# Conditioning rows of a two-block network: sums on VectorE alone, and the second layer's rows made in block 2's first feed-forward phase

## The chip, the cores and the metric

The kernel runs on one core of one Trainium2 chip. The metric is the device time of one execution in microseconds; three executions of the kernel before took 3672.66, 3673.09 and 3675.40 us, so 3673.09 in the median.

## What is computed (the reference)

A network of two blocks on 512 tokens of width 1024. Block 1 has two layers; each is a mixer (attention over dilated windows, a convolution and a pooling branch, gated and summed), a cross-attention over 256 memory tokens, and a feed-forward part with a causal convolution. Block 2 has two layers as well, on the same 512 tokens and on 256 context tokens. It is conditioned: from a vector c for the tokens and one c_ctx for the context come, per layer, six rows of 1024 each that shift, scale and gate the block's norms:

```python
for l in range(DEPTH):
    mx = (silu(c) @ ada_w[l] + ada_b[l]).reshape(bsz, 6, 1, d)
    mc = (silu(c_ctx) @ ada_w[l] + ada_b[l]).reshape(6, d)
    hx = modulate(rmsnorm_2(x, norm_g[l, 0]), mx[:, 0], mx[:, 1])
    ...                                      # mixer: yx, yc
    x = x + mx[:, 2] * rmsnorm_2(yx, norm_g[l, 1])
    hx = modulate(rmsnorm_2(x, norm_g[l, 2]), mx[:, 3], mx[:, 4])
    x = x + mx[:, 5] * rmsnorm_2(swiglu(hx, ffn_w13[l], ffn_w2[l]), norm_g[l, 3])
    ...                                      # the same for the context, with mc
```

The rows depend on c, c_ctx and the weights `ada_w` (2 x 1024 x 6144) alone, so they can be made at any time before block 2's layer uses them. All products are in float32, by splitting each operand into a high and a low part in TensorE's float32r format and adding three products.

## The kernel before

**Phases.** `run` (L1487) goes through block 1's phases `mix1`, `mem1`, `ffn1` twice, then block 2: `mix_ab`, `ffn2(0)`, `mix_mla`, `ffn2(1)`. In the feed-forward phases PSUM is four tiles of two banks (`open_ring`, L99). Every weight unit, 128 x 1024, comes through `wload` (L122): a DMA on SP's queue into one of three `raw` tiles, a copy to the high part on ScalarE (`whi`, L109), a subtraction for the low part on VectorE (`wlo`, L112), in one of five pairs of tiles. `mm3` (L133) is the three matmuls of a product. The compiler lays each engine's instructions in an order of its own, by the program's order and by what it holds to be ready; steps without a dependence on each other may be exchanged.

**A feed-forward phase** (`ffn1`, L826; `ffn2`, L1275) has 22 hidden chunks of 128, handled in parts of three to six chunks. For each chunk, two weight units are multiplied with the feature-major input (`projT`), the two results are combined (block 1: convolution at L530 and L533, Silu at L863, product at L865; block 2: Silu at L1314 and L1317, products at L1315 and L1318), and the result is split into `act` or `a` (L109 on ScalarE, L112 on VectorE). At the end of a part, `out_part` (L252) multiplies the part's chunks, for each token tile, with the rows of the down matrix, and VectorE adds the result to the running sums (L262). This is a part boundary: the first tile's last matmuls need the last chunk's `act`. `up_lead` (L815) makes the first two chunks' products while the input's tiles still come. With the last part come the norm and the residual's update (`postnorm`, L190), and the next phase's input.

**The conditioning rows** are made in `ffn1` by `ada_rows` (L908), in layer l of block 1 for layer l of block 2. One part is one of the six rows, for c and c_ctx at once. Per part, eight weight tiles `adaw` of 128 x 1024 come over SP's queue into two buffers, and two accumulators `acc0` (c) and `acc1` (c_ctx) take the tile times a number per partition:

```python
if kc == 0:
    nc.vector.tensor_scalar(acc[0], w, c[0], 1.0, op0=ALU.mult, op1=ALU.mult)           # L919
    nc.gpsimd.tensor_scalar(acc[1], w, c[1], 1.0, op0=ALU.mult, op1=ALU.mult)           # L920
else:
    nc.vector.scalar_tensor_tensor(acc[0], w, c[0], acc[0], op0=ALU.mult, op1=ALU.add)  # L922
    p = pool.tile([P, D], F32, name="adap")
    nc.gpsimd.tensor_scalar(p, w, c[1], 1.0, op0=ALU.mult, op1=ALU.mult)                # L924
    nc.gpsimd.tensor_tensor(acc[1], acc[1], p, op=ALU.add)                              # L925
```

Then TensorE sums over the partitions with four matmuls against ones (L938; 96 instructions in the profile over all parts), VectorE adds the bias (L939) and, for scales and gates, takes in the norm's gain (L941), and four small DMAs store the row in DRAM (L944). `mod_row` and `mod_col` (L947, L952) read it back where a phase needs it.

**What paces them.** `Fill` (L40) holds the generator. Each `yield 1` is one step and costs 1; after each chunk from the third on, `fill.run(3)` (L876) emits steps until what they cost is paid. A part is nine steps, a phase has 20 x 3 to pay with and 54 steps; what is left is drained before the last part's `out_part` (L879).

**The residual** `x` (four tiles of 128 x 1024) and, in block 2, `xc` (two tiles) lie on the right side of SBUF. `spill_x` (L285) stores them in DRAM and frees the room where a mixer needs it, `open_x` (L278) takes it again and loads them. In the feed-forward phases they stay in SBUF, though they are only read and written at the phase's two ends: `postnorm` adds to them as the last part's sums come.

Of the kernel before, what the change touches and what calls it, by code (L numbers as in the profile page):

```python
# [11 lines left out]
F32 = mybir.dt.float32  # L12
# [5 lines left out]
ALU = mybir.AluOpType  # L18
# [21 lines left out]
class Fill:  # L40
    """Work for TensorE, by key, that is laid between the steps of something with longer waits."""
# [37 lines left out]
class Net:  # L79
# [14 lines left out]
    def psum_pools(self, ctx, **bufs):  # L94
        """PSUM tiles under names of their own: of two banks for ps and S, of one for others."""
        pool = self.pool(ctx, "psum", space=PSUM)
        self.banks = {tag: (pool, n) for tag, n in bufs.items()}

    def open_ring(self):  # L99
        """All of PSUM as four tiles of two banks, from the end of one mixer to the next one."""  # L100
        self.ringctx = ExitStack()
        self.psum_pools(self.ringctx, ps=4)
# [19 lines left out]
    def wload(self, src, pool=None):  # L122
        """A weight unit as its two float32r parts."""
# [9 lines left out]
    def mm3(self, ps, l, r, first, last):  # L133
        """ps += l.T @ r, of operands that are given as (hi, lo)."""
# [10 lines left out]
    def rstd(self, src, n=D, junk=None):  # L145
        """1 / sqrt(mean of squares + eps) along the free axis."""
# [11 lines left out]
    def at(self, hT, t):  # L158
        """Columns of token tile t of (hi, lo), or of (hi, lo, hi, lo) with the context's tiles 4 and 5 apart."""
# [5 lines left out]
    def to_T(self, src, hT, t, shift=None, whole=False):  # L165
        """[128 tokens, 1024] -> columns t of the feature-major (hi, lo); shift [128, 8] is added by feature."""
# [23 lines left out]
    def postnorm(self, x, y, g, psum=False, last=False):  # L190
        """x += rmsnorm(y) * g"""
# [16 lines left out]
    def lead1(self, name, l):  # L208
        """The normalised and feature-major input of a phase, and what makes token tile t of it."""
# [5 lines left out]
    def lead2(self, l, i, hT, gp=None):  # L215
        """The same for block 2; hT may be what the phase before still reads other tiles of."""
# [11 lines left out]
    def ending(self, post, pre, lag=1):  # L228
        """What takes a phase's sums by token tile: the next phase's tiles begin as the residual's come,
        the last ones between that phase's first products."""  # L230
# [9 lines left out]
    def ready(self, t):  # L240
        """Token tile t of the phase's input, and those before it."""
# [3 lines left out]
    def projT(self, ps, unit, hT, kcs, col=0, n=S, w=P, off=0, first=True, last=True):  # L245
        """Feature-major product: ps[w, n] of a weight unit's columns and hT."""
# [5 lines left out]
    def out_part(self, acts, wsrc, tiles, yps, first, last, epi):  # L252
        """Token-major product of some feature chunks with the rows [128, 1024] of a matrix that belong
        to them; parts add up in yps, and epi(t, y) takes a tile's whole sum."""
# [30 lines left out]
    def spill_x(self, write=True):  # L285
        """Frees the tiles; returns where the residual comes back from."""
# [7 lines left out]
    def open_xc(self):  # L294
# [3 lines left out]
        for t in range(2):  # L298
            self.nc.sync.dma_start(self.xc[t], self.I["ctx_2"][t * P : (t + 1) * P])

# [42 lines left out]
    def masks1(self, pool):  # L343
        """For a query block: the keys of the first group in four tiles, then those of the others."""
# [3 lines left out]
    def tok_proj(self, hT, wsrc, tiles, n, evac, nk=KC, tags=("p",)):  # L348
        """Token-major product of hT with a column group of n; wsrc[u] holds two row chunks."""
# [38 lines left out]
    def nmax(self, sv, sink=None, mask=None):  # L388
        """Scores are kept as -scale * q.k: their least is minus the softmax's maximum. A mask is added first."""
# [9 lines left out]
    def exps(self, sv, nm, n, sink=None):  # L399
        """Unnormalised probabilities in SBUF and 1 / their sum."""  # L400
# [14 lines left out]
    def probs_T(self, Pt, nk):  # L415
        """Probabilities [p, nk * 128] -> [p, nk, 128] with the keys on partitions."""
# [15 lines left out]
    def pv_pair(self, o, PTs, vs):  # L432
        """o[64 h :, q] = v[h].T @ PT[h] of two heads side by side; vs(h, k) is a key chunk's values."""
# [1258 lines left out]
```

## Time and profile before

| | |
|---|---|
| Median of three runs | 3673.09 us (3672.66 to 3675.40) |
| Profiled execution, first to last instruction | 3670.9 us (no time of its own is given beside the span; the median is 2.2 us longer) |
| TensorE busy (PE) | 3552.0 us, 97% |
| VectorE busy (DVE) | 1954.7 us, 53% |
| ScalarE busy (ACT) | 1333.5 us, 36% |
| GpSimd busy (POOL) | 843.4 us, 23% |
| Moved by DMA | 357.75 MB, 97 GB/s over the span |

Times are in microseconds unless marked ns; start times count from the span's start. A row of a table of windows gives the stretch and its length, then the busy time of PE, PEld (weight loads), DVE, ACT and POOL in it, each with the number of instructions that began there, then TensorE's mean granted clock (1.00 is 2.4 GHz, 0.50 is 1.2 GHz), the mean busy share of the DMA engines, and GB/s. In a row of the order of time stand start, duration, engine, line, operation, output and inputs, shapes and, in brackets, for how long the engine was idle before and on what. L112 and L109 are lines of helpers; what they work on is told by the tiles' names. Matmuls overlap, so that the busy time of one is longer than the distance between two.

### The profile page before, as it was taken

To read this page: it belongs to the slowest core of one execution; us is meant where nothing else is said; L and a number is where in the kernel's file an instruction comes from. 1 tells how busy PE (TensorE), PEld (TensorE's weight loads), DVE (VectorE), ACT (ScalarE), POOL (GpSimd) and SP (SyncE) were. 2 spreads that over 40 slices of the span, in tenths; PEclk is the share of its full clock that TensorE was granted. 3 is DMA by queue.
4 is the path that set the end of the run, shared out by engine and by line. 5 is a ranking of instruction groups with operands and counts; after the bars stand their busy time and mean duration, and the time that the engine had idled before them with its cause. 6 is when DMAs were issued, how large, how long until landed. Compare 5 with 4: busy or idle time off the path is not lost.

```text
span 3670.9 us, 48470 instructions
## 1 busy us (share of the span) xinstructions
PE 3552.0 (97%) x19261; PEld 3009.1 (82%) x19261; DVE 1954.7 (53%) x2922; ACT 1333.5 (36%) x2372; POOL 843.4 (23%) x752
## 2 busy tenths in 40 slices
PE   8999999999999999989998999999999989999998
PEld 8877798777898778977777888788888888888887
DVE  4443356878644435579766567433333366653243
ACT  4342344222443324432224346432221256643222
POOL 0211124746102111256631112200000032220001
PEclk9999999999999999999999999999999999999999
DMA  4243234555322433355542110222211120122322
GB/s 127 80 131 97 87 110 145 172 165 156 112 75 82 132 96 119 123 169 180 160 127 89 35 41 24 87 70 74 64 64 58 53 93 21 36 81 83 96 95 89
DMA packets 108403, 357.75 MB, mean 97 GB/s; under 512 B 16424, under 2 KB 18016, under 8 KB 108176
## 3 DMA queue, kind: packets, MB, share of 16 engines
q1 hardware_dynamic: 108176, 354.65, 30.9%
q8 instruction: 151, 2.47, 0.3%
q14 instruction: 76, 0.62, 0.1%
HBM read 344.01 MB, written 10.58 MB: 97 GB/s over the span
## 4 chain that ended last, share of the span: by engine, by line
PE 85%; DVE 7%; issue 2%; ACT 2%; POOL 2%; DMA 1%; SPq 0%; ACTq 0%; POOLq 0%; DVEq 0%
PE ps L136 19%; PE ps L138 19%; PE ps L137 19%; PE p L136 4%; PE p L137 4%; PE p L138 4%; PE T L423 3%; PE p L437 3%; PE S L136 2%; DVE wlo L112 2%; PE S L137 1%; DVE acc L922 1%; PE S L138 1%; DVE t L533 1%; PE T L138 1%
## 5 line engine op out<-in xcount | busy, mean ns | idle before, releaser
L112 DVE TENSOR_TENSOR wlo<-raw,whi 128x1024 fp32r<-128x1024 f32 (+2 forms) x510 | 654.2, 1289 | 756.0 <-ACT whi L109 742.4
L109 ACT ACTIVATE whi<-raw 128x1024 fp32r<-128x1024 f32 (+2 forms) x510 | 517.8, 1018 | 1089.6 <-PE ps L137 644.6
L137 PE MATMUL ps<-hTlo,whi 128*128 128x512 f32 (+1 forms) x2048 | 758.0, 370 | 4.5 <-DVE hTlo L112 3.4
L136 PE MATMUL ps<-hThi,whi 128*128 128x512 f32 (+1 forms) x2048 | 758.7, 371 | 2.7 <-ACT hThi L109 1.4
L138 PE MATMUL ps<-hThi,wlo 128*128 128x512 f32 (+1 forms) x2048 | 757.2, 370 | 0.0
L136 PEld LDWEIGHTS ps<-hThi,whi 128*128 128x128 f32 x2048 | 386.3, 189 | 76.4 <-ACT whi L109 6.7
L137 PEld LDWEIGHTS ps<-hTlo,whi 128*128 128x128 f32 x2048 | 386.9, 189 | 69.4 <-DVE hTlo L112 4.0
L138 PEld LDWEIGHTS ps<-hThi,wlo 128*128 128x128 f32 x2048 | 386.7, 189 | 65.7
L925 POOL TENSOR_TENSOR acc<-acc,adap 128x1024 f32<-128x1024 f32 x84 | 235.1, 2799 | 7.0
L154 POOL TENSOR_SCALAR rstd<-ms 128x1 f32<-128x1 f32 x78 | 24.6, 315 | 823.5 <-ACT junk L152 808.1
L924 POOL TENSOR_SCALAR adap<-adaw,cs 128x1024 f32<-128x1024 f32 x84 | 159.2, 1895 | 106.1 <-DMA adaw<-in_ada_w_dram 100.7
L922 DVE SCALAR_TENSOR_TENSOR acc<-adaw,cs,acc 128x1024 f32<-128x1024 f32 x84 | 168.1, 2001 | 9.2 <-DMA adaw<-in_ada_w_dram 8.9
L136 PE MATMUL ps<-whi,act 128*128 128x512 f32 x352 | 148.7, 424 | 24.4 <-ACT act L109 24.4
L136 PE MATMUL p<-whi,hThi 128*128 128x384 f32 x464 | 162.8, 351 | 8.3 <-DVE y L262 3.5
L136 PE MATMUL ps<-whi,a 128*128 128x512 f32 x440 | 170.4, 392 | 0.0
L137 PE MATMUL ps<-wlo,a 128*128 128x512 f32 x440 | 170.4, 390 | 0.0
L138 PE MATMUL ps<-whi,a 128*128 128x512 f32 x440 | 170.4, 390 | 0.0
L413 POOL TENSOR_SCALAR g<-g,den 128x768 f32<-128x768 f32 (+3 forms) x88 | 74.4, 847 | 416.6 <-DVE den L409 373.2
L137 PE MATMUL p<-wlo,hThi 128*128 128x384 f32 x464 | 158.4, 341 | 3.1 <-DVE wlo L112 3.1
L262 DVE TENSOR_TENSOR y<-y,ps 128x1024 f32<-128x1024 f32 x88 | 106.9, 1217 | 101.8 <-PE ps L138 101.5
L138 PE MATMUL p<-whi,hTlo 128*128 128x384 f32 x464 | 158.1, 341 | 0.8 <-DVE hTlo L112 0.8
L138 PE MATMUL ps<-whi,act 128*128 128x512 f32 x352 | 147.2, 423 | 7.5 <-DVE act L112 7.5
(410 smaller groups left out, 7114.9 us busy)
## 6 DMA issues: line engine op xcount, KB each, us to landing
raw<-in_ffn_w_dram SPq DMA_DIRECT2D x132, 512.0 KB
adaw<-in_ada_w_dram SPq DMA_DIRECT2D x96, 512.0 KB
raw<-in_w_up_dram SPq DMA_DIRECT2D x88, 512.0 KB
raw<-in_w_gate_dram SPq DMA_DIRECT2D x48, 512.0 KB
raw<-in_w_down_dram SPq DMA_DIRECT2D x44, 512.0 KB
raw<-in_w_qkv_dram SPq DMA_DIRECT2D x48, 384.0 KB
raw<-in_w_conv_dram SPq DMA_DIRECT2D x18, 512.0 KB
raw<-in_ab_w_in_dram SPq DMA_DIRECT2D x24, 384.0 KB
```

Of the source, the lines that this page charges most:

```text
L109: return self.nc.scalar.activation(out, in_, AF.Copy, scale=scale)
L112: return self.nc.vector.tensor_tensor(out, a, b, op=ALU.subtract)
L136: mm(ps, lhsT=l[0], rhs=r[0], start=first, stop=False)
L137: mm(ps, lhsT=l[0], rhs=r[1], start=False, stop=False)
L138: mm(ps, lhsT=l[1], rhs=r[0], start=False, stop=last)
L262: self.nc.vector.tensor_tensor(yps[t], yps[t], y, op=ALU.add)
L413: self.nc.gpsimd.tensor_scalar(Pt, Pt, r, 1.0, op0=ALU.mult, op1=ALU.mult)
L423: nc.tensor.transpose(ps[:, k * P : (k + 1) * P], Pt[:, (k0 + k) * P : (k0 + k + 1) * P], self.ident)
L437: self.nc.tensor.matmul(o[64 * h : 64 * h + 64], lhsT=vs(h, k), rhs=PTs[h][:, k], start=k == 0, stop=k == nk - 1)
L922: nc.vector.scalar_tensor_tensor(acc[0], w, c[0], acc[0], op0=ALU.mult, op1=ALU.add)
L924: nc.gpsimd.tensor_scalar(p, w, c[1], 1.0, op0=ALU.mult, op1=ALU.mult)
L925: nc.gpsimd.tensor_tensor(acc[1], acc[1], p, op=ALU.add)
```

## The change

- `ada_rows` takes a list of parts, and both accumulators are made on VectorE: no instruction of it is left on GpSimd, and the tile `adap` is gone. The loads of the bias and the gain, the row sums and the bias addition become three steps where they were one, so that a part has ten steps.
- Block 1's two feed-forward phases make three parts each, all for block 2's first layer (0 to 2, then 3 to 5), with `fill.run(1.5)` after a chunk.
- The six parts of the second layer are made in `ffn2(0)`. After `up_lead`, the residual's six tiles (`xc`, `x`) are stored in DRAM and their room is taken by the conditioning tiles; `fill.run(4.2)` follows each chunk from the third on. After the 18th chunk's `act`, before the last part, what is left is drained, the room is given back and the residual is loaded again.

Docstrings and comments, which the change takes out as well, are left out here.

```diff
     def spill_x(self, write=True):
...
+    def spill_xc(self):
+        d = self.xcd.rearrange("(t p) d -> t p d", p=P)
+        for t in range(2):
+            self.nc.sync.dma_start(d[t], self.xc[t])
+        self.xcctx.close()
+        return d
+
-    def open_xc(self):
+    def open_xc(self, src=None):
...
-            self.nc.sync.dma_start(self.xc[t], self.I["ctx_2"][t * P : (t + 1) * P])
+            self.nc.sync.dma_start(self.xc[t], self.I["ctx_2"][t * P : (t + 1) * P] if src is None else src[t])
...
     def ffn1(self, l, hT, lead):
...
-            fill.add("ada", self.ada_rows(l, ap))
+            fill.add("ada", self.ada_rows(0, range(3 * l, 3 * l + 3), ap))
...
                     if f > 1:
-                        fill.run(3)
+                        fill.run(1.5)
...
-    def ada_rows(self, l, pool):
+    def ada_rows(self, l, parts, pool):
         nc, I = self.nc, self.I
-        for i in range(6):
+        for i in parts:
             acc = [pool.tile([P, D], F32, name=f"acc{r}") for r in range(2)]
             for kc in range(KC):
                 w = pool.tile([P, D], F32, name="adaw", bufs=2)
                 nc.sync.dma_start(w, I["ada_w_2"][l][kc * P : (kc + 1) * P, i * D : (i + 1) * D])
-                c = [self.cs[:, kc, r : r + 1] for r in range(2)]
-                if kc == 0:
-                    nc.vector.tensor_scalar(acc[0], w, c[0], 1.0, op0=ALU.mult, op1=ALU.mult)
-                    nc.gpsimd.tensor_scalar(acc[1], w, c[1], 1.0, op0=ALU.mult, op1=ALU.mult)
-                else:
-                    nc.vector.scalar_tensor_tensor(acc[0], w, c[0], acc[0], op0=ALU.mult, op1=ALU.add)
-                    p = pool.tile([P, D], F32, name="adap")
-                    nc.gpsimd.tensor_scalar(p, w, c[1], 1.0, op0=ALU.mult, op1=ALU.mult)
-                    nc.gpsimd.tensor_tensor(acc[1], acc[1], p, op=ALU.add)
+                for r in range(2):
+                    c = self.cs[:, kc, r : r + 1]
+                    if kc == 0:
+                        nc.vector.tensor_scalar(acc[r], w, c, 1.0, op0=ALU.mult, op1=ALU.mult)
+                    else:
+                        nc.vector.scalar_tensor_tensor(acc[r], w, c, acc[r], op0=ALU.mult, op1=ALU.add)
                 yield 1
...
+            for q in range(4):
+                rows, cols = slice(32 * q, 32 * q + 32), slice(q % 2 * 512, q % 2 * 512 + 512)
+                nc.sync.dma_start(bias[rows], ...)
+                if gi is not None:
+                    nc.sync.dma_start(ng[rows], ...)
+            yield 1
             ps = self.psum()[:, 0]
             for q in range(4):
...
+                nc.tensor.matmul(ps[rows], lhsT=self.ones, rhs=acc[q // 2][:, cols], start=True, stop=True, tile_position=(0, 32 * q))
+            yield 1
             nc.vector.tensor_tensor(bias, bias, ps, op=ALU.add)
...
-            yield 1
...
     def ffn2(self, l, hT, xs, parts, nact, lead):
...
+            fill, cada = Fill(), ExitStack()
...
                         self.up_lead(load, early, hT)
+                        if l + 1 < DEPTH:
+                            backc, back = self.spill_xc(), self.spill_x()
+                            fill.add("ada", self.ada_rows(l + 1, range(6), self.pool(cada, "ada", side="right")))
...
                     acts.append((a[:, 0], a[:, 1]))
+                    if f > 1:
+                        fill.run(4.2)
+                if l + 1 < DEPTH and f0 + n == NF - parts[-1]:
+                    fill.drain()
+                    cada.close()
+                    self.open_x(back)
+                    self.open_xc(backc)
+                    xs = self.x + self.xc
                 epi = None
```

## Rows read from the trace of the kernel before

**Rows 1.** The page's head: the span of the profiled execution.
```profile
span 3670.9 us, 48470 instructions
```

**Rows 2.** Windows: block 1's two feed-forward phases, then block 2's first.
```profile
575.00:920.00 345.00, 320.49 (x1408) 257.27 (x1407) 267.97 (x238) 96.24 (x117) 207.72 (x90) 0.95 0.53 161
...
1550.00:1910.00 360.00, 329.58 (x1414) 262.33 (x1413) 276.64 (x247) 99.61 (x120) 204.84 (x90) 0.93 0.53 163
...
2432.00:2860.00 428.00, 428.00 (x2267) 368.63 (x2266) 135.54 (x137) 92.31 (x112) 0.00 (x0) 1.00 0.21 67
```

**Rows 3.** Windows around TensorE's waits, one without a wait, and the lead-in.
```profile
684.00:704.00 20.00, 12.87 (x50) 8.55 (x49) 20.00 (x22) 4.99 (x7) 12.60 (x7) 0.83 0.55 181
768.00:784.00 16.00, 11.84 (x35) 8.62 (x34) 12.14 (x10) 1.26 (x2) 15.37 (x8) 0.68 0.54 154
832.00:844.00 12.00, 7.95 (x23) 5.60 (x22) 9.83 (x8) 1.26 (x2) 11.55 (x6) 0.72 0.44 137
890.00:903.00 13.00, 8.65 (x26) 6.08 (x25) 10.40 (x8) 1.26 (x2) 12.46 (x6) 0.74 0.44 113
1580.00:1606.00 26.00, 15.20 (x44) 11.47 (x43) 18.79 (x13) 3.92 (x5) 16.98 (x8) 0.67 0.67 199
1660.00:1674.00 14.00, 7.26 (x28) 4.26 (x27) 14.00 (x16) 3.73 (x5) 8.72 (x5) 0.76 0.59 178
1745.00:1759.00 14.00, 9.86 (x27) 7.04 (x26) 10.44 (x7) 1.26 (x2) 13.46 (x7) 0.63 0.47 137
1809.00:1821.00 12.00, 7.95 (x24) 5.54 (x23) 9.69 (x7) 1.26 (x2) 11.54 (x6) 0.72 0.41 132
1866.00:1879.00 13.00, 8.84 (x27) 6.26 (x26) 10.51 (x9) 1.26 (x2) 12.45 (x7) 0.74 0.45 125
...
616.00:636.00 20.00, 20.00 (x87) 15.97 (x86) 6.65 (x11) 7.68 (x10) 1.10 (x1) 1.00 0.24 76
...
574.00:592.00 18.00, 13.18 (x89) 12.45 (x89) 14.14 (x10) 3.52 (x5) 17.29 (x10) 0.81 0.48 147
```

**Rows 4.** Order of time at one part boundary: VectorE, then TensorE's first row after each wait.
```profile
764.12 2.97 DVE L112 TENSOR_TENSOR wlo<-raw,whi 128x1024 fp32r<-128x1024 f32 x1 [1.51 <-ACT whi L109]
...
768.58 3.07 DVE L922 SCALAR_TENSOR_TENSOR acc<-adaw,cs,acc 128x1024 f32<-128x1024 f32 x1
...
772.17 1.53 DVE L922 SCALAR_TENSOR_TENSOR acc<-adaw,cs,acc 128x1024 f32<-128x1024 f32 x1
773.63 2.84 DVE L112 TENSOR_TENSOR act<-t,act 128x512 fp32r<-128x512 f32 x1
...
772.96 0.80 PE L136 MATMUL ps<-whi,act 128*128 128x512 f32 x1 [3.10 <-ACT act L109]
...
776.53 0.79 PE L138 MATMUL ps<-whi,act 128*128 128x512 f32 x1 [1.06 <-DVE act L112]
```

**Rows 5.** Order of time on VectorE at the boundary without a wait.
```profile
619.51 1.21 DVE L112 TENSOR_TENSOR wlo<-raw,whi 128x1024 fp32r<-128x1024 f32 x1
...
624.43 0.69 DVE L112 TENSOR_TENSOR act<-t,act 128x512 fp32r<-128x512 f32 x1 [0.70 <-ACT act L109]
```

**Rows 6.** Instructions by line, whole span: least, median and longest in ns.
```profile
L922 DVE SCALAR_TENSOR_TENSOR acc<-adaw,cs,acc x84: 1270/1776/3520, 577.7 to 1887.3; 128x1024 f32<-128x1024 f32 x84
...
L919 DVE TENSOR_SCALAR acc<-adaw,cs x12: 743/1944/1959, 572.4 to 1853.6; 128x1024 f32<-128x1024 f32 x12
...
L925 POOL TENSOR_TENSOR acc<-acc,adap x84: 2348/2417/3462, 576.2 to 1889.7; 128x1024 f32<-128x1024 f32 x84
```

**Rows 7.** Windows: a stretch with one short wait of TensorE.
```profile
700.00:716.00 16.00, 15.61 (x69) 12.51 (x67) 14.57 (x10) 1.66 (x3) 13.53 (x7) 1.00 0.49 143
```

**Rows 8.** Order of time at a part boundary of block 2's first feed-forward phase.
```profile
2676.12 0.40 PE L136 MATMUL ps<-whi,a 128*128 128x512 f32 x1
...
2679.76 0.96 DVE L112 TENSOR_TENSOR a<-s,a 128x768 fp32r<-128x768 f32 x1 [0.91 <-ACT a L109]
2682.01 1.22 DVE L262 TENSOR_TENSOR y<-y,ps 128x1024 f32<-128x1024 f32 x1 [1.29 <-PE ps L138]
```

More of the change, by code (lines that the diff above doesn't have):

```diff
@@ L930, in ada_rows @@
                 ng = pool.tile([P, 512], F32, name="adag")
+            for q in range(4):
+                rows, cols = slice(32 * q, 32 * q + 32), slice(q % 2 * 512, q % 2 * 512 + 512)
+                nc.sync.dma_start(bias[rows], I["ada_b_2"][l, i * D + cols.start : i * D + cols.stop].partition_broadcast(32))
+                if gi is not None:
+                    nc.sync.dma_start(ng[rows], I["norm_g_2"][l, gi, cols].partition_broadcast(32))
+            yield 1
             ps = self.psum()[:, 0]
             for q in range(4):
-                r, h = q // 2, q % 2
-                rows, cols = slice(32 * q, 32 * q + 32), slice(h * 512, h * 512 + 512)
-                nc.sync.dma_start(bias[rows], I["ada_b_2"][l, i * D + h * 512 : i * D + h * 512 + 512].partition_broadcast(32))
-                if gi is not None:
-                    nc.sync.dma_start(ng[rows], I["norm_g_2"][l, gi, cols].partition_broadcast(32))
-                nc.tensor.matmul(ps[rows], lhsT=self.ones, rhs=acc[r][:, cols], start=True, stop=True, tile_position=(0, 32 * q))
+                rows, cols = slice(32 * q, 32 * q + 32), slice(q % 2 * 512, q % 2 * 512 + 512)
+                nc.tensor.matmul(ps[rows], lhsT=self.ones, rhs=acc[q // 2][:, cols], start=True, stop=True, tile_position=(0, 32 * q))
+            yield 1
             nc.vector.tensor_tensor(bias, bias, ps, op=ALU.add)
@@ L1497, in run @@
         self.xd = self.dram.tile([S, D], F32, name="xd")
+        self.xcd = self.dram.tile([256, D], F32, name="xcd")
         self.hp = self.pool(ctx, "hT")
```

## The prediction

> **What bounds the kernel now.** I read the page's head first: a span of 3670.9 us [rows 1], 2.2 us under the median of the three runs (3673.09). Then the table of windows over the phases that the change touches [rows 2]. In block 2's first feed-forward phase TensorE is busy for all 428 of 428 us at a granted clock of 1.00. In block 1's two feed-forward phases, where the conditioning rows are made, it is busy for 320.5 of 345 and 329.6 of 360 us at 0.95 and 0.93. TensorE is the bound, and it loses time only in the two phases with conditioning work in them.
>
> Third, narrow windows around the places where it waits [rows 3]. The first nine are part boundaries, where `out_part` begins and needs the last chunk's `act` (two of them, at 684 and 1660, with the row sums of L938 in front, which wait for VectorE's `acc`). A stretch without a loss, 616 to 636, gives the price of a matmul: 20/87 = 0.230 us. The nine windows are 140 us long and hold 284 matmuls, which at that price are 65.3 us: **74.7 us are lost**, 30.2 in the first layer and 44.5 in the second. TensorE was idle for 140 - 90.4 = 49.6 of these; in the rest it ran at the lower of its clocks (1.2 instead of 2.4 GHz) after a wait: mean grants of 0.63 to 0.83. The stretch 616 to 636 is a boundary too, with GpSimd idle but for 1.1 us, and it loses nothing.
>
> Fourth, the order of time at one boundary [rows 4]. After the up products, the last chunk's chain on VectorE holds a weight split of 2.97 us, an `acc` step of 3.07 and one of 1.53, and the `act` split of 2.84. TensorE waits 3.10 us for the chunk's high part and 1.06 for its low part. The two splits took 1.21 and 0.69 at the boundary without a loss [rows 5]. So the cause is VectorE instructions that take two to four times their time beside GpSimd's `acc` and `adap`: an `acc` step of VectorE is 1.27 at the least and 1.78 in the median, GpSimd's sum 2.42 [rows 6].
>
> **The change, part by part.**
>
> *Sums on VectorE alone.* Per part of 8 weight tiles, VectorE had 1 scaling and 7 `acc` steps and GpSimd 1 and 14; now VectorE has 2 and 14. Over 12 parts GpSimd loses 180 instructions, and VectorE goes from 96 to 192: 24 x 0.74 + 168 x 1.27 = 231 us, at the minimum durations [rows 6], since nothing on GpSimd stands beside them any more. The weight loads (12 x 8) and the row sums stay in number.
>
> *Half of it out of block 1.* Each of its phases makes three parts instead of six: 6 scalings and 42 steps on VectorE, 58 us. TensorE's row sums of six parts move along; what they take there is taken off here.
>
> What this is worth at a boundary, by rows 4 to 6: the weight split falls by 1.7 us, the two `acc` steps by 1.8 and 0.3, the `act` split by 2.1, 5.9 us in all, against 4.2 of wait. If each place now holds two sums instead of one, 2 x 1.27 = 2.5 come back and 0.8 of wait is left. A short wait has no slow clock behind it: 700 to 716 holds one of about 0.4 and is granted 1.00 [rows 7]. I take 0.8 us for each of the nine places, 7 in all: **-68 us**. The bounds: 0 left (-75), or half the loss left (-37), if the sums crowd the chain more. A wait of 4.8 us with its clock, at the first layer's lead-in (574 to 592) [rows 3], has two `acc` steps in front too; I count no gain, and keep 5 for the range.
>
> *The second layer's rows in block 2's first feed-forward phase.* VectorE has 135.5 us of work in 428 [rows 2] and gets 12 x 0.74 + 84 x 1.27 = 116 more, 251 of 428 with the six parts' small bias steps still to add. GpSimd is at 0.0 there, so nothing stretches. What can be hurt is again the boundary, six of them with sums around: the up products end at 2676.1, the last chunk's split is done at 2680.7 [rows 8], and TensorE lost nothing. But it had no time to spare: VectorE takes up the first tile's whole sum at 2682.0, and that tile's last six matmuls, which need the late chunk, take 6 x 0.230 = 1.4 us, so they began about when the split ended. One sum in front of a step of the chain costs up to 1.27. Bounds: 0, and a boundary like those of rows 3 (7 us each, 42 in all). I take 1.2 us for each of six, near the first, as here nothing stretches the sums: **+7**.
>
> *Transfers.* Six stores and six loads of 512 KB for the residual, 48 of the weights, and the small ones of six parts: some 34 MB more in 428 us at 67 GB/s, hence about 147, under the 161 and 163 that the two other phases move [rows 2]. On SP's queue the first conditioning load waits for the stores, because it takes the residual's room; behind it stand weight loads. Six stores at 67 to 163 GB/s are 19 to 47 us; none of the weight loads needs that room, so they can go between, and the sums aren't wanted until the phase's end. The way back waits for the last row's store, with the loads of the last four chunks behind it; 16 chunks x 4.2 pay for 67 steps where there are 60, so the sums end before it, and the residual is first needed when the last part's sums end, over 60 us later. I take **+1** for both, with 0 and 20 as bounds.
>
> Sum: -68 + 7 + 1 = **-60 us**: a span of 3611, and 3613 with the 2.2 us around it.
>
> **Rivals.**
>
> *A. The sums themselves are what is late, not what GpSimd does to them.* VectorE was busy for 268 of 345 us [rows 2], more than GpSimd with 208, and the change gives all work to it. At a boundary of rows 4 it would decide once some five further sums (5.9/1.27) stand in the chain: then nothing is won in block 1, and the six boundaries of block 2 cost 7 each: 3673 + 42 = **3715**. For it: sums do stand in the chain now. Against it: without the stretching VectorE's work falls there in spite of the second row's sums (84 `acc` steps in the two phases as now, at 1.27 instead of a median of 1.78). The Trainium skill speaks for this side: Perfetto Trace Analysis, Optimizing Scalar/DVE Operations, says that where VectorE is saturated, handing work to ScalarE or even GpSimd may make sense; the change does the reverse, and by that rule the time is A's 3715. The same passage warns that the two share a read port, so that a hand-over between them might not help, and the rows (2.97 beside 1.21) are on the side of the warning. I give A 6 in 100.
>
> *B. Block 2 gives it all back.* Its phase has no slack in TensorE. If each of the six boundaries costs 11 us, between the 8.5 and the 15.9 of the longest of rows 3, block 1's gain is used up: 3673 - 68 + 66 = **3671**. Against it: GpSimd is idle. 4 in 100.
>
> *C. The residual's way out and back, or crowding, costs 20 to 45 us* on top: **3633 to 3658**. For it: SP's queue is in order, and no stretch of the trace has such a swap inside a busy phase. 15 in 100.
>
> *D. No wait left at all*, the lead-in's too: 3673 - 75 - 5 = **3593**. 10 in 100. That the change doesn't do what it says (sums left on GpSimd) the diff excludes.
>
> **How the numbers follow.** The forecast, 3613 with its own bounds of 3595 to 3632, has 65 in 100; with D and most of C the range is **3586 to 3655**. A measurement of this kernel can tell some 0.2%, 7 us, from no change. Faster by more: forecast, C and D, 0.90; within it: 0.04, B; slower: 0.06, A.
>
> **What would show it.** Right: GpSimd nearly idle in both of block 1's feed-forward phases; weight splits at 1.22 to 1.23 and `acc` steps at 1.27 throughout; clock 0.98 or more in the windows of rows 2 for block 1; those phases together some 70 us shorter; block 2's phase no more than 15 us longer. Wrong: waits of TensorE for `act` or for `acc` of over 2 us at the boundaries although every step has its minimum duration (A); idle time or a lower clock in block 2's phase (B); TensorE waiting for `whi` or `wlo` behind a weight load just after the residual's stores or loads (C).

## Result and profile after

| | before | after |
|---|---|---|
| median of 4 runs each (lowest to highest), us | 3674.24 (3672.66 to 3675.75) | 3590.88 (3587.88 to 3594.31) |
| profiled execution, us | see the table ahead of the rows | 3594.31, the longest of its four |

The ratio of the times is 0.9777, with a 95% interval of 0.9766 to 0.9789: **faster by 83 us, 2.2%**. The forecast was 3613, some 60 us faster; the time lies inside the range, 22 us below the forecast and near rival D's 3593.

The head of the profile of the changed kernel: its span, and busy time, share and instructions of each engine.

```profile
span 3592.5 us, 48260 instructions
## 1 busy us (share of the span) xinstructions
PE 3519.9 (98%) x19261; PEld 2994.1 (83%) x19261; DVE 1917.2 (53%) x3018; ACT 1335.5 (37%) x2372; POOL 429.1 (12%) x572
```

GpSimd has lost its 180 instructions. VectorE has 96 more than before and is busy for less time.

Windows of the changed kernel over the three phases of [rows 2] (length; busy time of PE, PEld, DVE, ACT, POOL with instructions; granted clock; DMA share; GB/s):

```profile
566.00:913.00 347.00, 346.12 (x1626) 286.15 (x1625) 219.74 (x267) 114.78 (x141) 3.19 (x5) 1.00 0.45 139
...
1491.00:1838.00 347.00, 346.31 (x1629) 286.85 (x1628) 220.53 (x267) 115.40 (x142) 3.39 (x5) 1.00 0.46 146
...
2360.00:2741.00 381.00, 380.29 (x2027) 323.29 (x2027) 207.87 (x204) 79.53 (x96) 0.00 (x0) 1.00 0.41 130
```

In both phases of block 1 TensorE is now idle for under 1 us where it was idle for 25 and 30 [rows 2], and its granted clock is 1.00 where it was 0.95 and 0.93. VectorE is at 220 us where it was at 268 and 277. In block 2's phase TensorE has stayed full beside 208 us of VectorE in 381.

To compare phases of kernels whose times are shifted, I measure a phase of block 1 from the memory part's last product with `oT` to the last part's first down product, and block 2's from the first part's first down product to the last part's:

| us | block 1, layer 1 | block 1, layer 2 | block 2, `ffn2(0)` |
|---|---|---|---|
| before | 389.7 | 399.1 | 465.2 |
| after | 347.1 | 346.3 | 472.8 |
| difference | -42.6 | -52.8 | +7.6 |

The spans differ by 78.4 us: 42.6 + 52.8 - 7.6 = 87.8 in these phases, less 9.4 in stretches that do the same work in both kernels (5.8 of it behind the last part's first down product of `ffn2(0)`). A second profiled execution of the changed kernel had a span of 3587.3 us with the same phases (347.5, 346.3, 473.1), so some us outside the phases are the difference of two executions.

Five of the nine boundaries of [rows 3], in windows of the changed kernel:

```profile
679.00:699.00 20.00, 20.00 (x88) 16.04 (x87) 7.84 (x10) 3.96 (x5) 0.00 (x0) 1.00 0.11 35
747.00:767.00 20.00, 20.00 (x90) 16.38 (x89) 11.26 (x13) 4.51 (x6) 0.00 (x0) 1.00 0.33 95
802.00:822.00 20.00, 20.00 (x90) 16.19 (x87) 18.88 (x22) 5.29 (x7) 0.00 (x0) 1.00 0.48 141
...
1539.00:1559.00 20.00, 20.00 (x89) 16.40 (x88) 14.96 (x17) 7.38 (x9) 0.00 (x0) 1.00 0.79 263
1605.00:1625.00 20.00, 20.00 (x89) 16.34 (x88) 8.93 (x11) 4.48 (x6) 0.00 (x0) 1.00 0.07 27
```

Each of the nine has TensorE busy for 20 of 20 us at 1.00, with VectorE between 7.8 and 19.0. The order of time on VectorE at the boundary that answers to [rows 4] shows what is in the chain (start, duration, engine, line, operation, tiles; idle time before it in brackets):

```profile
748.10 1.22 DVE L112 TENSOR_TENSOR wlo<-raw,whi 128x1024 fp32r<-128x1024 f32 x1
749.23 1.65 DVE L540 SCALAR_TENSOR_TENSOR t<-ps,cw,t 128x384 f32<-128x384 f32 x4
750.80 1.27 DVE L930 SCALAR_TENSOR_TENSOR acc<-adaw,cs,acc 128x1024 f32<-128x1024 f32 x1
751.99 0.68 DVE L872 TENSOR_TENSOR t<-t,ps 128x512 f32<-128x512 f32 x1
753.37 0.69 DVE L112 TENSOR_TENSOR act<-t,act 128x512 fp32r<-128x512 f32 x1 [0.70 <-ACT act L109]
```

The weight split fell from 2.97 to 1.22, the `acc` steps from 3.07 and 1.53 to one of 1.27, the `act` split from 2.84 to 0.69. By line over the whole span (least, median, longest in ns), the sums have no spread left:

```profile
L930 DVE SCALAR_TENSOR_TENSOR acc<-adaw,cs,acc x168: 1272/1279/1286, 576.9 to 2676.7; 128x1024 f32<-128x1024 f32 x168
...
L928 DVE TENSOR_SCALAR acc<-adaw,cs x24: 744/748/755, 573.2 to 2649.5; 128x1024 f32<-128x1024 f32 x24
```

What TensorE's rows still name as a wait (total us, times, longest): block 1's first phase, then block 2's lead-in (2300 to 2340), then its phase.

```profile
PE ps L136 <- ACT hThi L109: 0.7, 1, 0.7
PE ps L137 <- DVE hTlo L112: 0.2, 1, 0.2
...
PE ps L137 <- DVE hTlo L177: 3.5, 1, 3.5
...
PE ps L136 <- ACT a L109: 0.7, 1, 0.7
```

No wait for `act` or `acc` is left at any part boundary of block 1 (in its second phase TensorE names the 0.7 us for `hThi` alone). The one wait of size is new, and lies ahead of block 2's phase. The 0.7 us for `a` lie at the fifth of block 2's boundaries. There a sum stands on VectorE in front of the chunk's last product:

```profile
2665.93 1.28 DVE L930 SCALAR_TENSOR_TENSOR acc<-adaw,cs,acc 128x1024 f32<-128x1024 f32 x1 [1.40 <-DMA adaw<-in_ada_w_dram]
2667.13 0.41 DVE L1329 TENSOR_TENSOR s<-s,ps 128x256 f32<-128x256 f32 x1
```

### The profile page after: what moved, and what is told of

Read it like the earlier page. It is cut to its first block, busy times and chain, and to the rows that moved or that the text cites. A ratio compares the mean times of both kernels' runs of the same rounds, so it can differ in the third digit from the quotient of the medians.

```text
span 3592.5 us, 48260 instructions
## 1 busy us (share of the span) xinstructions
PE 3519.9 (98%) x19261; PEld 2994.1 (83%) x19261; DVE 1917.2 (53%) x3018; ACT 1335.5 (37%) x2372; POOL 429.1 (12%) x572
## 4 chain that ended last, share of the span: by engine, by line
PE 90%; DVE 3%; ACT 2%; POOL 2%; DMA 1%; issue 1%; SPq 0%; ACTq 0%; POOLq 0%; DVEq 0%
PE ps L136 21%; PE ps L137 21%; PE ps L138 21%; PE p L136 4%; PE p L137 4%; PE p L138 4%; PE T L430 3%; PE p L444 3%; PE S L136 2%; PE S L137 1%; PE S L138 1%; DMA adaw<-in_ada_w_dram 1%; PE T L138 1%; PE T L136 1%; PE T L137 1%
## 5 line engine op out<-in xcount | busy, mean ns | idle before, releaser
L112 DVE TENSOR_TENSOR wlo<-raw,whi 128x1024 fp32r<-128x1024 f32 (+2 forms) x510 | 603.8, 1190 | 734.6 <-ACT whi L109 719.3
L930 DVE SCALAR_TENSOR_TENSOR acc<-adaw,cs,acc 128x1024 f32<-128x1024 f32 x168 | 209.4, 1279 | 14.6 <-DMA adaw<-in_ada_w_dram 14.3
L262 DVE TENSOR_TENSOR y<-y,ps 128x1024 f32<-128x1024 f32 x88 | 106.6, 1218 | 85.7 <-PE ps L138 85.4
L136 PE MATMUL ps<-whi,act 128*128 128x512 f32 x352 | 138.2, 395 | 0.0
L137 PE MATMUL ps<-wlo,act 128*128 128x512 f32 x352 | 137.2, 392 | 0.0
L138 PE MATMUL ps<-whi,act 128*128 128x512 f32 x352 | 136.3, 390 | 0.0
L109 ACT ACTIVATE PT<-T 128x384 f32<-128x384 f32 (+2 forms) x160 | 74.4, 465 | 111.6 <-PE T L430 109.6
```

The lines of the kernel that those rows point to most:

```text
L109: return self.nc.scalar.activation(out, in_, AF.Copy, scale=scale)
L112: return self.nc.vector.tensor_tensor(out, a, b, op=ALU.subtract)
L136: mm(ps, lhsT=l[0], rhs=r[0], start=first, stop=False)
L137: mm(ps, lhsT=l[0], rhs=r[1], start=False, stop=False)
L138: mm(ps, lhsT=l[1], rhs=r[0], start=False, stop=last)
L262: self.nc.vector.tensor_tensor(yps[t], yps[t], y, op=ALU.add)
```

## Experiments

Line numbers are each kernel's own: the changed kernel's `acc` steps are L930, its row sums L945. Times are medians; the phases are those of the table above.

**1. VectorE alone, nothing moved.** Theory: GpSimd's work stretches VectorE's instructions, and that is the whole loss. Rival (A): the number of sums on VectorE is what is late. This kernel leaves all twelve parts in block 1, so VectorE has twice the sums there that it has in the changed kernel.

```diff
-            fill.add("ada", self.ada_rows(0, range(3 * l, 3 * l + 3), ap))
+            fill.add("ada", self.ada_rows(l, range(6), ap))
...
-                        fill.run(1.5)
+                        fill.run(3)
...
-                        if l + 1 < DEPTH:
-                            backc, back = self.spill_xc(), self.spill_x()
-                            fill.add("ada", self.ada_rows(l + 1, range(6), self.pool(cada, "ada", side="right")))
...
-                if l + 1 < DEPTH and f0 + n == NF - parts[-1]:
-                    fill.drain()
-                    cada.close()
-                    self.open_x(back)
-                    self.open_xc(backc)
-                    xs = self.x + self.xc
```

> VectorE alone makes the sums, but all six parts of each layer stay in block 1's phases (steps paid with 3 a chunk) and nothing is made or swapped in block 2. Theory 'stretching' (GpSimd's conditioning work stretches VectorE's instructions beside it, and that alone made TensorE wait): 3585 to 3605 us, close to the changed kernel's 3591; acc steps at 1.27 to 1.29, weight splits at 1.22, no wait of TensorE for act above 2 us. Rival 'amount' (too many sums in block 1's phases, whoever makes them): 3630 to 3674, with waits for act at the part boundaries although each step has its least duration.

Measured: 3603.87 us (4 runs), against 3672.07 of the kernel before beside it; ratio 0.9812 [0.9797, 0.9827]. Phases 361.2, 357.4 and 465.3. The durations, the window of the first phase, TensorE's waits for VectorE's sums in the first and the second phase, and the window of 20 us in front of one of these waits:

```profile
L930 DVE SCALAR_TENSOR_TENSOR acc<-adaw,cs,acc x168: 1269/1277/1286, 577.9 to 1863.3; 128x1024 f32<-128x1024 f32 x168
```

```profile
566.00:927.00 361.00, 354.45 (x1646) 287.93 (x1644) 274.29 (x322) 115.64 (x143) 3.06 (x5) 0.99 0.54 172
```

```profile
PE ps L945 <- DVE acc L930: 4.9, 2, 2.5
...
PE ps L945 <- DVE acc L930: 4.6, 2, 2.6
```

```profile
905.30:925.30 20.00, 17.61 (x80) 14.27 (x80) 19.17 (x22) 7.22 (x10) 0.00 (x0) 0.99 0.54 180
```

Taking GpSimd out gives 68 of the 83 us by itself, with every sum still in block 1 and VectorE as busy as before (274 of 361). No wait for `act` is left. So rival A falls as the cause of the loss, and the change's two halves part as 68 and 13 us (3604 to 3591, from two series of runs). What block 1 still loses beside the changed kernel, 14.1 and 11.1 us, is the six further row sums (one of them takes TensorE some 1.09 us, 6.5 in all, about 5.5 of it inside the measured stretches) and four waits of a row sum for a late `acc`, 9.5 us; most of the other 10 us I put to the lower clock behind these waits (0.95 in 898 to 928), which I did not divide. Here something of A is real: in the 20 us in front of each of the four waits VectorE is busy for 19.0 to 19.5, with every step at its least duration. At twice the changed kernel's number of sums they do come late, but for the row sums alone.

**2. The move alone, one accumulator on GpSimd as before.** The mirror of run 1: it asks whether the stretching follows GpSimd into a phase that TensorE fills.

```diff
-                for r in range(2):
-                    c = self.cs[:, kc, r : r + 1]
-                    if kc == 0:
-                        nc.vector.tensor_scalar(acc[r], w, c, 1.0, op0=ALU.mult, op1=ALU.mult)
-                    else:
-                        nc.vector.scalar_tensor_tensor(acc[r], w, c, acc[r], op0=ALU.mult, op1=ALU.add)
+                c = [self.cs[:, kc, r : r + 1] for r in range(2)]
+                if kc == 0:
+                    nc.vector.tensor_scalar(acc[0], w, c[0], 1.0, op0=ALU.mult, op1=ALU.mult)
+                    nc.gpsimd.tensor_scalar(acc[1], w, c[1], 1.0, op0=ALU.mult, op1=ALU.mult)
+                else:
+                    nc.vector.scalar_tensor_tensor(acc[0], w, c[0], acc[0], op0=ALU.mult, op1=ALU.add)
+                    p = pool.tile([P, D], F32, name="adap")
+                    nc.gpsimd.tensor_scalar(p, w, c[1], 1.0, op0=ALU.mult, op1=ALU.mult)
+                    nc.gpsimd.tensor_tensor(acc[1], acc[1], p, op=ALU.add)
```

> The move alone: c_ctx's sums stay on GpSimd, three parts in each of block 1's phases, six in block 2's first feed-forward phase with the residual stored meanwhile. 'Stretching': block 1 keeps about half of its stalls and block 2's phase, which had none, gets some at its part boundaries: 3630 to 3680 us, weight splits of up to 3.4 us in both. 'Amount': 3590 to 3605, as the changed kernel.

Measured: 3669.33 us (10 runs); ratio 0.9988 [0.9979, 0.9998]. Phases 361.7, 368.6 and 513.8: block 1 gains 58.5, and block 2 gives 48.6 back. From the lead-in to the end of block 2's phase, TensorE's longest waits, and the groups of VectorE in 2400 to 2745 (count, busy us, mean ns, idle time before):

```profile
PE ps L136 <- ACT a L109: 21.7, 3, 12.4
PE ps L138 <- DVE a L112: 7.4, 4, 2.9
PE ps L137 <- DVE hTlo L177: 6.4, 1, 6.4
```

```profile
L930 DVE SCALAR_TENSOR_TENSOR acc<-adaw,cs,acc 128x1024 f32<-128x1024 f32 x35 | 74.7, 2134 | 15.5 <-DMA adaw<-in_ada_w_dram 15.3
...
L112 DVE TENSOR_TENSOR wlo<-raw,whi 128x1024 fp32r<-128x1024 f32 x37 | 62.9, 1705 | 70.6 <-ACT whi L109 70.5
...
L112 DVE TENSOR_TENSOR a<-s,a 128x768 fp32r<-128x768 f32 x12 | 26.7, 2223 | 4.6 <-ACT a L109 4.6
```

The stretching comes along: an `a` split takes 2.22 us, `acc` 2.13 with half the sums of the changed kernel. One wait for `a` alone is 12.4 us, and the lead-in's for `hTlo` 6.4. (Not all of the 12.4 is stretching: in front of it VectorE also idles for 3.7 us, waiting for a weight tile `adaw` with the chunk's own product behind that sum.) The move without the change of engine is worth next to nothing, and the loss belongs to GpSimd's presence, not to block 1.

**3. What of GpSimd's work stretches.** Runs 1 and 2 leave open whether it is GpSimd's reads, its writes, or only the hand-over of `adap` and `acc`. Two kernels give GpSimd work that nobody uses, on a tile of its own, in block 1's phases of the changed kernel; the one rescales the tile (reads and writes), the other fills it (writes only).

```diff
+        if l == 0:
+            scr = pool.tile([P, D], F32, name="scr")
+            nc.gpsimd.memset(scr, 0.0)
...
+                if l == 0:
+                    for _ in range(4):
+                        nc.gpsimd.tensor_scalar(scr, scr, 1.0, 1.0, op0=ALU.mult, op1=ALU.mult)
```

In the second kernel the last line is `nc.gpsimd.memset(scr, 0.0)`.

> The changed kernel with idle GpSimd work put back: in block 1's phases, at each weight tile, four scalings in place of a 128x1024 tile that nothing else uses (about 24 x 4 x 2 us a phase, as much as GpSimd had before). The sums stay on VectorE. 'Stretching': acc steps, weight and act splits take up to 3.4 us again and TensorE waits at the part boundaries: 3630 to 3680 us. 'Amount', or a dependence on GpSimd's results as the cause: 3588 to 3597, since nobody waits for this work.

> The same with four fills of the tile in place of the four scalings: GpSimd only writes, reads nothing. If any GpSimd work stretches VectorE: as the scalings, in proportion to GpSimd's busy time. If it is the shared read side of SBUF that stretches (GpSimd reading while VectorE has two inputs from SBUF): acc steps stay at 1.27 to 1.29 and the time at 3588 to 3600 us.

Measured, one run each: 3630.53 us with reads, 3594.57 with fills alone (3672.41 for the kernel before beside them). Phases 367.1, 369.0, 472.8 with reads; 352.0, 346.8, 473.0 with fills. The groups from 566 to 700 us, with reads:

```profile
L936 POOL TENSOR_SCALAR scr<-scr 128x1024 f32<-128x1024 f32 x86 | 125.1, 1455 | 7.0
...
L112 DVE TENSOR_TENSOR wlo<-raw,whi 128x1024 fp32r<-128x1024 f32 x22 | 38.5, 1763 | 28.4 <-ACT whi L109 28.4
L933 DVE SCALAR_TENSOR_TENSOR acc<-adaw,cs,acc 128x1024 f32<-128x1024 f32 x14 | 25.2, 1822 | 0.2 <-DMA adaw<-in_ada_w_dram 0.2
L540 DVE SCALAR_TENSOR_TENSOR t<-ps,cw,t 128x384 f32<-128x384 f32 (+3 forms) x29 | 12.2, 475 | 0.0
L112 DVE TENSOR_TENSOR act<-t,act 128x512 fp32r<-128x512 f32 x7 | 9.8, 1394 | 0.7 <-ACT act L109 0.7
```

The same groups with fills:

```profile
L936 POOL MEMSET scr<- 128x1024 f32 x96 | 92.7, 966 | 5.4
...
L112 DVE TENSOR_TENSOR wlo<-raw,whi 128x1024 fp32r<-128x1024 f32 x21 | 25.6, 1223 | 38.1 <-ACT whi L109 37.8
L933 DVE SCALAR_TENSOR_TENSOR acc<-adaw,cs,acc 128x1024 f32<-128x1024 f32 x14 | 17.6, 1278 | 1.2 <-DMA adaw<-in_ada_w_dram 1.2
L540 DVE SCALAR_TENSOR_TENSOR t<-ps,cw,t 128x384 f32<-128x384 f32 (+3 forms) x32 | 13.3, 475 | 1.3 <-ACT t L537 1.2
L112 DVE TENSOR_TENSOR act<-t,act 128x512 fp32r<-128x512 f32 x8 | 5.5, 686 | 1.4 <-ACT act L109 1.4
```

The scaling that begins each accumulator has one tensor operand, `adaw`. Over the whole span with fills (least, median, longest in ns):

```profile
L931 DVE TENSOR_SCALAR acc<-adaw,cs x24: 742/748/1519, 571.8 to 2652.1; 128x1024 f32<-128x1024 f32 x24
```

The windows of the same 134 us, with reads and then with fills:

```profile
566.00:700.00 134.00, 118.45 (x589) 100.58 (x588) 97.73 (x89) 43.81 (x54) 126.81 (x90) 0.94 0.43 134
```

```profile
566.00:700.00 134.00, 131.45 (x652) 111.75 (x651) 77.47 (x96) 45.28 (x57) 93.51 (x100) 0.97 0.43 137
```

Beside reads the weight split takes 1763 ns in the mean, `acc` 1822 and the `act` split 1394; beside fills, with GpSimd busy for 94 of 134 us (70%, more than the 60% of [rows 2]), they take 1223, 1278 and 686, as in the changed kernel. So, for instructions with two tensor operands in SBUF, it is GpSimd work that reads SBUF, whoever uses the result; work that reads without writing was not run. The convolution step (L540, a mean over its four shapes), one of whose two tensors comes from PSUM (`ps`), stays at 475 ns in both. The scaling, with its one tensor operand in SBUF, is less clear: of the twelve in block 1's phases, four with reads take 0.93 to 1.53 us and two with fills 1.02 and 1.52, the others about their least. The Trainium skill states the main finding, SBUF — State Buffer, section Who interferes with whom: a VectorE instruction with two SBUF inputs contends with a GpSimd instruction that reads SBUF, not with one that only writes it, and one with at most one SBUF input, outside the 2-port perf modes, does not contend. The two runs agree with the first half (1763 beside 1223 ns), and the convolution step with the second; the stretched scalings would have to be in such a mode to fit it, and no row tells the mode of an instruction.

The times of the two kernels hold one thing more. GpSimd also makes a small step of the norm (`rstdx`, L155) in the lead-in of block 1's phases, and there it stands behind the idle work. With reads TensorE then waits for `big`, which needs that step, 4.5 us in layer 1:

```profile
PE ps L169 <- DVE big L187: 4.5, 1, 4.5
```

In layer 2 that wait is 4.2 us. From the memory part's last product to the first down product the two layers take 58.2 and 58.6 us with reads, 52.8 and 48.0 with fills, 48.4 and 48.0 in the changed kernel. So of the 20.0 and 22.7 us by which the phases with reads are longer, about 10 each lie in the lead-in, where this delay has a part. The others lie behind it, where TensorE's longest waits are 6.3 and 7.8 us for `act`. Of the fills' 4.9 us in layer 1, 4.3 lie in the lead-in: `rstdx` stands behind six fills and starts 10.7 us after the memory part's last product, 7.5 in the changed kernel. What stretching costs is therefore read from the durations and from run 1, not from this run's 3630.53.

**4. What the sums that remain cost.** Each kernel leaves out seven of the eight weight tiles of every part, in block 1's phases or in block 2's; parts, row sums and residual transfers stay.

```diff
-            for kc in range(KC):
+            for kc in range(KC if l else 1):
```

```diff
-            for kc in range(KC):
+            for kc in range(1 if l else KC):
```

> The changed kernel with only the first of the eight weight tiles of each part loaded and summed in block 1 (leaves out 7/8 of the first layer's conditioning sums; the row sums over partitions stay). 'Stretching': the sums left in block 1 cost nothing there, so its two phases last as in the changed kernel (352.5 and 351.8 us from the last products of the memory part to the last part's first) within 3 us, 3583 to 3594 us in all. 'Crowding' (VectorE's sums still cost at the boundaries): shorter by 10 us or more.

> The same for block 2: only the first of eight weight tiles of each part of the second layer is loaded and summed (leaves out 7/8 of those sums); the residual is still stored and loaded again. If the sums cost block 2's phase what its lengthening shows (472.8 us against 465.2 before from the first to the last part's first down product), it falls to 471 to 472, the six row sums being the rest; and the wait of 3.5 us in front of it (hTlo behind acc steps) goes: 3580 to 3590 us.

Measured, one run each: 3594.92 and 3585.52 us. Phases 346.5, 346.5, 473.0 and 347.4, 346.3, 472.8, hence the changed kernel's within 0.6 us; the first kernel's total is 0.9 us above what was expected, outside these phases. (The 352.5 and 351.8 in the expectation count from the start of the memory part's last products, 5.4 us earlier; 347.1 and 346.3 are the same stretches here.) The first kernel's window over block 1's first phase; then a stretch of block 2's phase, in the second kernel and in the changed one:

```profile
566.00:909.00 343.00, 342.31 (x1600) 282.94 (x1599) 168.79 (x223) 111.30 (x136) 1.42 (x3) 1.00 0.34 107
```

```profile
2440.00:2741.00 301.00, 301.00 (x1598) 258.88 (x1597) 99.71 (x101) 58.11 (x73) 0.00 (x0) 1.00 0.23 76
```

```profile
2440.00:2741.00 301.00, 300.29 (x1605) 255.50 (x1605) 176.72 (x172) 56.60 (x69) 0.00 (x0) 1.00 0.44 139
```

VectorE's sums cost the phases next to nothing: without 77 us of them in 301, TensorE gains its one wait of 0.7 us. Most of the 7.6 us by which block 2's phase is longer is TensorE's own work, in the changed kernel six row sums of some 1.09 us, 6.5. Of the other 1.1, 0.9 lies in the fifth part, behind the boundary with the wait of 0.7 us for `a`. Run 5 bears this out: it has the six row sums and no such wait, and its phase takes 471.9. The second kernel's 472.8 is the same number in part by accident: one of its row sums lies ahead of the phase, and a row sum in it waits 0.9 us for a scaling. The second kernel's wait for `hTlo` at the lead-in fell from 3.5 to 0.7 us, which points to the sums in front of it, and to the last run.

**5. Order of the steps.** Rival for what run 1 still waited for: the change cuts a part's end into three steps, so that the row sums come a step after the last sum. This kernel undoes the cut alone.

```diff
-            yield 1
             ps = self.psum()[:, 0]
...
-            yield 1
             nc.vector.tensor_tensor(bias, bias, ps, op=ALU.add)
...
+            yield 1
```

> The changed kernel with the bias loads, the row sums and the bias addition again in one step as before. 'Stretching': within 5 us of the changed kernel's 3591, since TensorE waited 6.7 us for acc in front of the row sums only because VectorE's steps were stretched. Rival 'order' (the row sums put a step later is what took that wait away): waits of several us in front of row sums come back, 3600 to 3630.

Measured: 3588.85 us (4 runs); ratio 0.9774 [0.9759, 0.9788], phases 347.1, 346.5, 471.9, and no wait of a row sum. The three steps are worth nothing measurable with three parts a phase. They don't explain run 1's waits either, since run 1 has them; there VectorE was full in front of each wait.

**6. Holding the second layer's sums back.** In the changed kernel they begin in the lead-in. VectorE there, at the end of TensorE's wait of 3.5 us for `hTlo`, which ends at 2330.51:

```profile
2327.71 2.48 DVE L930 SCALAR_TENSOR_TENSOR acc<-adaw,cs,acc 128x1024 f32<-128x1024 f32 x2 [2.69 <-DMA adaw<-in_ada_w_dram]
2330.11 1.12 DVE L177 SCALAR_TENSOR_TENSOR hTlo<-ps,modcol,hThi 128x128 fp32r<-128x128 f32 x4
```

The edit makes the sums' coefficients depend on the first chunk's product, adding zero times it:

```diff
+                    if f == 0 and l + 1 < DEPTH:
+                        cs = self.const.tile([P, KC, 2], F32, name="cs2")
+                        nc.vector.scalar_tensor_tensor(cs, s[:, :16].rearrange("p (k r) -> p k r", r=2), 0.0, self.cs, op0=ALU.mult, op1=ALU.add)
+                        self.cs = cs
                     a = ap.tile([P, 2, nt * P], R, name="a")
```

> The changed kernel with the second layer's sums held back: they read a copy of the conditioning numbers that is made from the first chunk's product s (times zero), so that none of them can stand on VectorE between the lead-in's hTlo steps. If the wait of 3.5 us in front of block 2's first feed-forward phase and the slow clock after it come from acc steps there, both go: 3 to 6 us under the changed kernel run beside it, and no new waits in the phase. If they come from something else, or if the same number of steps in less room costs as much at the boundaries: within 2 us of it.

> The changed kernel once more, beside the one with the sums held back: 3588 to 3594 us.

Measured: 3590.26 us (4 runs), ratio 0.9773 [0.976, 0.9786]; the changed kernel beside it 3592.32 (5 runs), 0.9783 [0.9769, 0.9796]. The lead-in's window and wait in this kernel, then the window in the changed kernel's first profile:

```profile
2310.00:2345.00 35.00, 33.89 (x257) 32.39 (x257) 15.43 (x24) 9.77 (x18) 0.00 (x0) 1.00 0.32 103
```

```profile
PE ps L137 <- DVE hTlo L177: 0.7, 1, 0.7
```

```profile
2310.00:2345.00 35.00, 31.02 (x239) 30.28 (x237) 25.39 (x31) 8.45 (x16) 0.00 (x0) 0.95 0.61 189
```

The wait goes, the granted clock there is 1.00 for 0.95, and the stretch from block 1's end to `ffn2(0)`'s first down product falls from 522.2 us (the changed kernel beside it) to 517.9; the phase behind it grows by 1.2. So the expectation came true for the wait and the clock, and not for the total: the 2 us between the medians are less than the 3 to 6 named and lie inside the runs' spread, so a gain in the total is not shown. No kernel of these is measurably better than the changed one.

## Why the prediction was right, and where its sum was off

The sign, the mechanism and the order of size held. Point by point:

- **What bounds it, and the cause.** TensorE's waits at the part boundaries, made by VectorE instructions that GpSimd stretched: shown by runs 1, 2 and 3. The predicted durations (1.22 to 1.23 for splits, 1.27 for `acc`) came out as 1.22 at the boundary shown and 1.27 to 1.29 throughout.
- **Block 1's boundaries, -68.** This term was mis-sized. The phases fell by 42.6 + 52.8 = 95.4 us, of which 6.5 are the row sums that moved, so 88.9 stand against 67.5. The step that was off is "If each place now holds two sums instead of one, 2 x 1.27 = 2.5 come back and 0.8 of wait is left". Its premise was wrong on the kernel's own count: a step now makes two sums on VectorE instead of one, but 1.5 steps follow a chunk instead of 3, so that a phase has 42 `acc` steps before and after, and the chain of [rows 4] held two of them already. Nothing was left at any of the nine: at the boundary shown, a single sum of 1.27 stands in the chain, and VectorE is through with it in time to idle 0.70 us for ScalarE's high part of `act`. That is 7.2 us (9 x 0.8). The lead-in, counted at no gain, gave up 3.9 of its 4.8 us of wait (0.7 and 0.2 are left) and 2.0 more with the lower clock behind it [rows 3]: from the memory part's last product to the first down product, layer 1 takes 48.4 us where it took 54.3 (layer 2: 48.0 in both). The 16 narrow row-sum matmuls in the windows were priced at 0.230 us where 8 take 1.09, which hid 1.5. The other 7 us lie between the windows of [rows 3], which were too narrow; I did not divide them further.
- **"what they take there is taken off here".** The size was left out, and it hid two real terms that cancel: 6.5 us off block 1, 6.5 onto block 2.
- **Block 2's boundaries, +7.** The phase grew by 7.6, but not for the reason given: 6.5 of it is the row sums. The number was right by luck. As a wait, the term measured 0.7 to 0.9: the 1.2 us for each of six places supposed a sum in the way at every one, and it was in the way at one (2665.93).
- **The residual's transfers, +1.** TensorE has no wait in the phase but the 0.7 for `a`. Rival C did not occur.
- **Not foreseen:** the sums start in the lead-in to `ffn2(0)`, ahead of the phase, and put `hTlo` back by 3.5 us (run 6). The prediction had looked at block 1's lead-in alone.

Of the rivals, A is excluded as the cause by run 1, and its rule that work handed to GpSimd relieves a busy VectorE does not hold here: VectorE is busy for 1915.6 us of run 1's span without the help and for 1954.7 with it. What is left of A is run 1's four waits of the row sums. B is about what the move alone does (run 2: 48.6 us given back). D came nearest: no wait was left in block 1. Its small chance rested on the 0.8 us per place, which were an upper guess for a chain that in fact had slack once it was unstretched.

With the terms as measured the sum is -88.9 in block 1, the row sums cancelling, +1.1 in block 2's phase and +0.5 in the stretch between the two (522.0 us before, 522.5 after): -87.3. The medians differ by 83; the 4 us between lie in stretches with the same work, and the two profiled executions of the changed kernel differ by 5 in them. In the stretch between, run 6 puts the lead-in's loss at 4.3 us. What makes up for it lies in the first 52 us behind block 1's phase: up to the last product into `T` of `wlo` and `hThi` they take 52.1 us before and 48.2 in the changed kernel's first profile, with a wait of 1.0 us for `big` and a stretch at the lower clock less. That need not be the change's doing: the second profile takes 49.6 there, and the kernels with fills and with seven eighths of block 1's sums left out take 51.2 and 51.9.

## What to carry to other kernels

When an instruction of VectorE shows a wide spread in a trace (1.27 at the least, 1.8 in the median), look at what GpSimd reads meanwhile, and count the stretched time of everything else on VectorE before handing GpSimd a share: here GpSimd's half of the sums cost 68 us more than the same sums on VectorE, where they cost nothing with three parts a phase and four waits, 9.5 us, with six. Look first at the short instruction that a full TensorE waits for in order, since a stretch of 2 us there is a wait at each part and a lower clock behind it. Once stretched durations are gone, recompute a chain from the least durations with its own waits (here for ScalarE) before leaving a remainder, count from the program how many sums a chunk gets before and after, and price narrow matmuls by their own rows.

## What the runs showed of the hardware

- GpSimd's fills (966 ns for 128x1024) leave VectorE's two-tensor SBUF instructions at their least; its rescaling in SBUF raises the mean of a 1.22 us split to 1.76 and of a 0.69 us split to 1.39. The VectorE instructions of these windows with a tensor operand in PSUM stay as they are beside either (475 ns for the convolution steps, 1218 and 1219 for `y<-y,ps` in 566 to 915). A scaling with one tensor operand in SBUF, 0.74 us at the least, reached 1.53 beside rescalings and 1.52 beside fills.
- The longest excess is about as long as one instruction of GpSimd. Beside sums of 2.35 us at the least, `acc` goes from 1.27 up to 3.52 us (2.25 more) and the `act` split from 0.68 to 2.90 (2.2 more); beside rescalings of 1.04, they go up to 2.07 and 1.53 (0.8 more each):

```profile
L933 DVE SCALAR_TENSOR_TENSOR acc<-adaw,cs,acc x168: 1269/1278/2069, 582.1 to 2715.8; 128x1024 f32<-128x1024 f32 x168
```

- The stretching is mutual. Of GpSimd's 192 rescalings, the 119 with a weight split, an `act` split or an `acc` step beside them have a median of 1.89 us, the 33 beside an idle VectorE one of 1.05 and at most 1.07. All of them (least, median, longest over the run's span):

```profile
L936 POOL TENSOR_SCALAR scr<-scr x192: 1043/1154/2091, 566.0 to 1653.7; 128x1024 f32<-128x1024 f32 x192
```

- VectorE can be busy for 274 of 361 us beside a TensorE at a clock of 0.99 (run 1), and in a 20 us window for 18.88 (802 to 822) without a wait of TensorE. Its busy share did not tell whether it was late; the durations in the chain did.
